# A short tile's residual by an accumulating transfer, and a later square for the thirteenth tile, in a gated encoder step

## Chip, cores and metric

The kernel runs on one core of a Trainium2 chip. The metric is the device time of one execution in microseconds (us); less is better. Five engines work side by side, each through its own queue of instructions in a fixed order: TensorE (PE, matrix products; PEld is its loading of weights), VectorE (DVE), ScalarE (ACT), GpSimd (POOL) and SyncE (SP, which here only issues transfers). GpSimd issues transfers too, among them those that add to what the destination holds ("accumulating transfers").

## The reference

One step of an encoder layer on 2048 rows of a new stream (the prompt) and 32 rows of a running one (the sample), of width D = 1024, in float32. The parts of `reference.py` that matter:

```python
def rmsnorm(x, g):
    x32 = x.astype(jnp.float32)
    y = x32 * lax.rsqrt(jnp.mean(x32 * x32, axis=-1, keepdims=True) + EPS)
    return (y * g.astype(jnp.float32)).astype(x.dtype)

def layer(h, p, conv_hist, pool_hist, pos, g_mix, w_in, conv_w, conv_b, pool_w, pool_scale,
          w_out, g_ple, w_ple_gate, w_ple):
    hn = rmsnorm(h, g_mix)
    proj = hn @ w_in
...
    h = h + jnp.concatenate([yA, yB], axis=-1) @ w_out
    gate = jax.nn.sigmoid(rmsnorm(h, g_ple) @ w_ple_gate)
    h = h + (p @ w_ple) * gate
    return h, new_conv, new_pool
...
    return rmsnorm(h, g_final), jnp.stack(convs, 0), jnp.stack(pools, 0)
```

Between `proj` and the output projection stand a short gated convolution (512 channels) and a pooling mixer (512 channels), whose last rows are returned as new states. The change concerns only the last two lines of the layer and the closing norm: `h + (p @ w_ple) * gate`, and `rmsnorm(h, g_final)`.

## The kernel before

**Tiles.** The rows are cut into sixteen tiles of 128 rows (0 to 15) and a short one of 32 rows, the sample (number 16, `NT - 1`). Each stage of the layer passes over all tiles and leaves its result in DRAM: `h_d` holds the rows after the output projection, `e_d` the product `p @ w_ple`. The change lies in the last stage, the gate stage, which runs from about 730 us to the end.

**Products.** A float32 product is made of three products of parts: `split` (lines 81 and 84) lets ScalarE cast a tile to its high part and VectorE subtract that from the tile, which leaves the low part, and `FINE` names the three pairs of parts that are multiplied. Two tiles of rows (a pair) go through `seven`, Strassen's scheme in Winograd's form: seven products of half tiles with half weights in place of eight, each of twelve matmuls of 128x128 by 128x512. In the first six of them stand the "steps" 1 to 6, at which other work is put into the program. The sums of rows that the scheme needs (S1 to S4) are made by `prep_g` for the next pair while this pair runs: VectorE transposes the two `hn` tiles (line 1560), then sums, then splits. Of each product, `carry` copies a first part out of PSUM (line 1573, ScalarE), and `out` adds the second (line 1581, VectorE), takes the sigmoid (line 1582, or 1579 where there is only one part), and multiplies `e` by it (line 1584, VectorE). Then comes `h`: line 1590 has GpSimd issue a transfer that adds the rows of `h_d` to `e` in place, so that `e` becomes the new `h`; where a tile's `h` has been loaded, VectorE adds `e` to it instead (line 1587).

**Closing norm.** `sumsq` (line 94, ScalarE) squares a finished tile and sums its rows, GpSimd turns the sum into the reciprocal root (lines 73 and 77), and `done_g` (line 1597, VectorE) scales the tile and sends it to the output (line 1600; GpSimd's queue, for tiles 12 to 15 SyncE's). `finishing` makes these four steps (square and scale of either tile) and the loop joins them to the steps 4, 5, 5 and 6 of the next pair.

**Order.** The loop takes the pairs 0, 2, ... 12 (named by their first tile); pair 14 is `last_pair`, in which the thirteenth tile (number 12) has its square at step 3 (`square0`) and its scale at step 4 (`scale0`); the last tiles are finished by hand in `end` (lines 1640 to 1667). After the pairs 0, 2 and 4 the short tile takes one step each: its load, its transposes and parts, its products (`plain`, without Strassen) with everything that follows them. A scheduler sorts the instructions of each engine; those that are marked `keep_in_program_order` (the squares and scales with `later=True`, the transposes, everything `fixed`) hold their order among themselves.

**Buffers.** Tiles come from rings, and an allocation waits for the last use of the tile that had the buffer. In the gate stage the ring `ya` has five buffers for the `e` of all pairs from 2 on and for the `e` of the short tile; the ring `xh` has six for the `hn` of the coming pairs (loaded by quarters, line 1512) and for an `h` that is loaded. Loads of `e` are line 396 on SyncE's queue. The names in the profile are those of the tiles; `x_g`, `y_g` and `z_g` are the PSUM banks of the seven products, `c_g` the copies, `x_gl` and `c_gl` those of the short tile.

Of the kernel before, what the change touches and what calls it, by code (L numbers as in the profile page):

```python
# [12 lines left out]
ALU = mybir.AluOpType  # L13
PSUM = bass.MemoryType.PSUM

P = 128
D = 1024
KC = D // P
SEQ = 2048
# [9 lines left out]
NT = SEQ // P + 1  # L29
# [7 lines left out]
def trunk(ctx, tc, x_p, x_s, c_conv, c_pool, p_p, p_s, g_mix, w_in, conv_w, conv_b, pool_w,  # L37
          pool_scale, w_out, g_ple, w_gate, w_ple, g_fin, y_p, y_s, sc_p, sp_p, sc_s, sp_s):
    nc = tc.nc
# [6 lines left out]
    h_d = tc.dram_tile([T, D], F32, name="h_d")  # L46
# [295 lines left out]
    def plain(name, A, W, n, carry, out):  # L342

        X, Y, Z = (bank(f"{c}_{name}") for c in "xyz")
        packed(X, A[0], W["11"], n, True)
        c2 = carry(X, (0, 1))
        packed(Z, A[0], W["T1"], n, True)
        packed(Z, A[1], W["22"], n, False)
        out(Z, c2, (0, 1))
        packed(X, A[1], W["21"], n, False)  # L350
        out(X, None, (0, 0))
# [41 lines left out]
    def load_rows(pool, name, i, pr, sa=None, queue=nc.sync):  # L393
        r, n = tiles[i]
        t = ring4(pool, f"{name}_{i}")
        queue.dma_start(t[:n], pr[r:r + n] if sa is None else rows_of(pr, sa, r, n))
        return t
# [906 lines left out]
    with ExitStack() as s2:  # L1304
# [263 lines left out]
        def gate_ops(h, e, n, name, i):  # L1568
            scale = lambda at: rs_h[:n, i + at[0]:i + at[0] + 1]

            def carry(ps, at):
                t = st.tile([P, NH], F32, tag="t", name=f"c_{name}_{at[0]}{at[1]}")
                carried.append(nc.scalar.copy(t[:n], ps[:n]))  # L1573
                return t

            def out(ps, c, at):
                if c is None:
                    c = st.tile([P, NH], F32, tag="t", name=f"g_{name}_{at[0]}{at[1]}")
                    nc.scalar.activation(c[:n], ps[:n], AF.Sigmoid, scale=scale(at))
                else:  # L1580
                    nc.vector.tensor_tensor(c[:n], ps[:n], c[:n], op=ALU.add)
                    nc.scalar.activation(c[:n], c[:n], AF.Sigmoid, scale=scale(at))
                ee = half_of(e, at, n)
                nc.vector.tensor_tensor(ee, ee, c[:n], op=ALU.mult)
                if h is not None and h[at[0]] is not None:
                    hh = half_of(h, at, n)
                    nc.vector.tensor_tensor(hh, hh, ee, op=ALU.add)
                elif at[0] + at[1] == 1:
                    r = tiles[i + at[0]][0]
                    nc.gpsimd.dma_start(e[at[0]], h_d[r:r + P], accum_op=ALU.add)  # L1590

            return carry, out
# [8 lines left out]

        def short_ops(h, e, n):

            carry1, out1 = gate_ops([h], [e], n, "gl", NT - 1)

            def carry(ps, at):
                t = carry1(ps, at)
                nc.vector.tensor_tensor(t[:n], ps[n:2 * n], t[:n], op=ALU.add)
                return t

            def out(ps, c, at):
                if c is None:
                    c = carry1(ps[n:2 * n], at)
                else:
                    nc.vector.tensor_tensor(c[:n], ps[n:2 * n], c[:n], op=ALU.add)
                out1(ps, c, at)

            return carry, out

        def last_pair(i, A, square0, scale0, square1, scale1):  # L1620
# [78 lines left out]
            def rest():  # L1699
                of_first(cols_of(0), nc.gpsimd)  # L1700
# [33 lines left out]
                weigh(1, cols_of(0))  # L1734
                normed(1, root(1))

            seven(f"g{i}", A, W, held, out, {1: lambda: (chunk(), square1()), 2: scale1, 3: square0, 4: lambda: (scale0(), rest()), 5: upper_half}, first_tile=True, end=end)

        def prep_g(i, ahead=False):

# [67 lines left out]
        def short_gate():  # L1808
            n = tiles[NT - 1][1]
            t = load_rows(ya, "hn", NT - 1, h_d)  # L1810
            yield
            A = short("gl", turned(NT - 1, t), n)
            h, e = (load_rows(*a) for a in ((xh, "h", NT - 1, h_d), (ya, "e", NT - 1, e_d)))
            yield
            plain("gl", A, W, n, *short_ops(h, e, n))
            done_g(NT - 1, h)
            yield

        def finishing(i, out):
            steps = []  # L1820
# [12 lines left out]
        def joined(a, b):  # L1833
            def both(p, q):
                def run():
                    p()
                    q()
                return run
            return {**a, **{st: both(a[st], f) if st in a else f for st, f in b.items()}}

        short_steps = short_gate()
        for i in range(0, NT - 3, 2):
            A = S.pop(i)
            following = prep_g(i + 2, not i)
            e = [load_rows(ya if i else xh, "e", i + b, e_d) for b in range(2)]
            h = [None, load_rows(xh, "h", i + 1, h_d)] if i == NT - 5 else None
            if i:
                for at, f in zip((4, 5, 5, 6), finish):
                    following = joined(following, {at: f})
            seven(f"g{i}", A, W, *gate_ops(h, e, P, f"g{i}", i), following)  # L1850
            finish = finishing(i, e if h is None else [e[0], h[1]])
            if i in (0, 2, 4):
                next(short_steps)
        last_pair(NT - 3, S[NT - 3], *finish)

# [27 lines left out]
```

## Time and profile before

| | |
|---|---|
| time, median of 3 runs | 907.2 us (907.12 to 908.23) |
| time of the profiled execution | 910.51 us |
| its span in the profile | 908.7 us, mean granted TensorE clock 0.996 |
| busy share of the span | PE 98%, PEld 79%, DVE 77%, ACT 50%, POOL 18% |
| moved by DMA | 198.51 MB, 218 GB/s over the span |
| gate stage | about 730 us to the end |
| TensorE's last product | ends at 901.4 us, 7.3 us ahead of the span's end |

The times of the runs are taken without the profiler; the profiled execution has a time of its own, and its span, from the first recorded instruction to the last, is what all positions below are counted in. A position such as 889.22 is in microseconds from the start of that span. A row of a timeline gives the start, the duration, the engine and line, the operation, the tiles written and read with their shapes, how many instructions were put together, and in brackets the idle time of the engine just before and what ended it. A row of the DMA view ends with the time from issue to landing. Matmuls overlap a little, so the durations of neighbouring rows add up to slightly more than the time between their starts.

### The profile page before, as it was taken

The page shows a single profiled execution, that of the slowest core. Times are in us where ns is not written, and L with a number is a line of the kernel's source. Part 1 is how long each engine was busy: PE and PEld are TensorE (multiplying, and loading weights), DVE is VectorE, ACT ScalarE, POOL GpSimd, SP SyncE. Part 2 cuts the span into 40 slices and gives each one's busy share as a digit, 9 for nine tenths or more (in the row PEclk, how much of TensorE's full clock was granted, in tenths as well). Part 3 has the DMA queues.
Part 4 walks back from the last instruction along what each step waited for, and adds up shares of the span by engine and source line. Part 5 has one row for each costly group of instructions (what it writes and reads, how often), then busy time and mean ns, then how long its engine had stood idle before and what let it go on. Part 6 is the DMA issues. An engine that isn't in the chain of part 4 may idle for free. (4 is left out here: it accounts for less than half of the span.)

```text
span 908.7 us, 12069 instructions
## 1 busy us (share of the span) xinstructions
PE 890.5 (98%) x4118; PEld 717.2 (79%) x4118; DVE 695.5 (77%) x1139; ACT 452.6 (50%) x820; POOL 166.5 (18%) x303
## 2 busy tenths in 40 slices
PE   8999999999999999999999999999999999999995
PEld 6788888888888888877788886888888788778884
DVE  6899799897993688846668579956466987688784
ACT  7744554554453354533444365544334865445453
POOL 2210122222121123100000020211111202214222
PEclk9999999999999999999999999999999999999998
DMA  8255286847699776667745496787677985698874
GB/s 273 57 188 173 83 259 204 248 157 225 178 339 427 174 225 196 215 222 235 255 137 172 164 343 192 251 256 259 204 261 271 306 264 116 155 216 228 219 212 176
DMA packets 116411, 198.51 MB, mean 218 GB/s; under 512 B 13510, under 2 KB 73982, under 8 KB 115453
## 3 DMA queue, kind: packets, MB, share of 16 engines
q1 hardware_dynamic: 92461, 117.91, 41.5%
q0 software_dynamic: 21440, 75.44, 26.6%
q10 hardware_dynamic: 2448, 4.39, 1.3%
q8 instruction: 32, 0.52, 0.2%
q14 instruction: 30, 0.25, 0.1%
HBM read 132.53 MB, written 65.15 MB: 218 GB/s over the span
## 5 line engine op out<-in xcount | busy, mean ns | idle before, releaser
L185 PE MATMUL z_g<-wg,g_S 128*128 128x512 f32 x192 | 48.1, 400 | 2.4 <-ACT c_g L1573 2.4
L185 PE MATMUL z_o<-wo,y_S 128*128 128x512 f32 x192 | 47.4, 389 | 0.0
L646 PE MATMUL x_zab<-B,w_zab_S 128*128 128x512 f32 x192 | 46.8, 391 | 0.2 <-DVE w_zab_S L84 0.2
L646 PE MATMUL z_zab<-B,w_zab_S 128*128 128x512 f32 x192 | 46.7, 391 | 0.0
L185 PE MATMUL x_o<-wo_T,y_S 128*128 128x512 f32 x192 | 46.5, 391 | 0.1
L185 PEld LDWEIGHTS z_g<-wg,g_S 128*128 128x128 f32 x192 | 36.4, 192 | 11.6 <-ACT c_g L1573 4.1
L185 PE MATMUL x_o<-wo,y 128*128 128x512 f32 x192 | 45.3, 390 | 0.1
L646 PEld LDWEIGHTS x_zab<-B,w_zab_S 128*128 128x128 f32 x192 | 35.8, 188 | 8.8 <-DVE w_zab_S L84 0.6
L185 PEld LDWEIGHTS x_o<-wo,y 128*128 128x128 f32 x192 | 36.0, 188 | 8.2 <-issue 0.5
L185 PEld LDWEIGHTS x_o<-wo_T,y_S 128*128 128x128 f32 x192 | 35.8, 188 | 8.3 <-DVE c_o L1319 0.9
L646 PEld LDWEIGHTS z_zab<-B,w_zab_S 128*128 128x128 f32 x192 | 35.8, 188 | 7.8 <-DVE w_zab_S L84 0.3
L185 PEld LDWEIGHTS z_o<-wo,y_S 128*128 128x128 f32 x192 | 36.0, 188 | 7.6 <-issue 0.2
L646 PE MATMUL x_ch<-B,w_ch_S 128*128 128x512 f32 x168 | 41.9, 392 | 0.0
L646 PE MATMUL x_zbv<-B,w_zbv_S 128*128 128x512 f32 x168 | 40.8, 392 | 0.0
L646 PE MATMUL z_zbv<-B,w_zbv_S 128*128 128x512 f32 x168 | 40.4, 390 | 0.0
L646 PE MATMUL z_ch<-B,w_ch_S 128*128 128x512 f32 x168 | 40.4, 389 | 0.0
L646 PEld LDWEIGHTS x_zbv<-B,w_zbv_S 128*128 128x128 f32 x168 | 31.3, 188 | 7.5 <-ACT V L986 0.4
L646 PEld LDWEIGHTS x_ch<-B,w_ch_S 128*128 128x128 f32 x168 | 31.3, 188 | 7.3 <-issue 0.4
L646 PEld LDWEIGHTS z_ch<-B,w_ch_S 128*128 128x128 f32 x168 | 31.5, 188 | 6.6
L646 PEld LDWEIGHTS z_zbv<-B,w_zbv_S 128*128 128x128 f32 x168 | 31.5, 188 | 6.5
L81 ACT CAST y_S<-y_fS 128x512 fp32r<-128x512 f32 x28 | 17.0, 619 | 26.3 <-PE x_o L185 12.2
L1373 POOL DMA_DIRECT2D gs<-in_w_ple_gate_dram x16 | 11.4, 716 | 87.9 <-DMA g_d<-gs 49.4
(559 smaller groups left out, 2271.5 us busy)
## 6 DMA issues: line engine op xcount, KB each, us to landing
wn<-in_w_in_dram SPq DMA_DIRECT2D x24, 512.0 KB, 5.0
y<-y_d SPq DMA_DIRECT2D x16, 512.0 KB, 7.0
hn<-h_d SPq DMA_DIRECT2D x61, 128.0 KB, 5.0
p_dT<-T POOLq DMA_DIRECT2D x15, 512.0 KB, 4.8
e<-e_d SPq DMA_DIRECT2D x15, 512.0 KB, 7.0
x<-in_x_prompt_dram SPq DMA_DIRECT2D x14, 512.0 KB, 5.3
e<-h_d POOLq DMA_DIRECT2D x13, 512.0 KB, 7.6
B<-p_d POOLq DMA_DIRECT2D x3, 2048.0 KB, 15.8
```

What stands on the lines that cost most here:

```text
L81: ins = nc.scalar.copy(hi, src)
L185: nc.tensor.matmul(ps[:n], lhs[:, k, a, :n], w[b][:, k], start=start and k + q == 0, stop=k == KH - 1 and q == 2, skip_group_check=True)
L646: nc.tensor.matmul(ps, lhs[:, k, x], b[:, k, y], start=start and k + q == 0, stop=stop and k == KH - 1 and q == 2, skip_group_check=True)
L1373: ins = nc.gpsimd.dma_start(t, rows[:, :, half * NH:half * NH + NH])
```

## The change

The short tile no longer loads its `h`. After its products an accumulating transfer adds the 32 rows of `h_d` to its `e`; its square goes into step 4 of pair 6, its scale and output into step 5 of that pair. The two additions of line 1587 with 32 rows are gone, and the `e` of the short tile is used a pair longer than before. In the last pair the square of tile 12 moves from step 3 to step 5, ahead of the gating of the last tile's upper half, and its scale from step 4 to step 6.

```diff
--- before.py
+++ after.py
@@ -1585,7 +1585,7 @@
                 if h is not None and h[at[0]] is not None:
                     hh = half_of(h, at, n)
                     nc.vector.tensor_tensor(hh, hh, ee, op=ALU.add)
-                elif at[0] + at[1] == 1:
+                elif n == P and at[0] + at[1] == 1:
                     r = tiles[i + at[0]][0]
                     nc.gpsimd.dma_start(e[at[0]], h_d[r:r + P], accum_op=ALU.add)
@@ -1601,7 +1601,7 @@
         def short_ops(h, e, n):
-            carry1, out1 = gate_ops([h], [e], n, "gl", NT - 1)
+            carry1, out1 = gate_ops(h, [e], n, "gl", NT - 1)
@@ -1734,7 +1734,7 @@
-            seven(f"g{i}", A, W, held, out, {1: lambda: (chunk(), square1()), 2: scale1, 3: square0, 4: lambda: (scale0(), rest()), 5: upper_half}, first_tile=True, end=end)
+            seven(f"g{i}", A, W, held, out, {1: lambda: (chunk(), square1()), 2: scale1, 4: rest, 5: lambda: (square0(), upper_half()), 6: scale0}, first_tile=True, end=end)
@@ -1810,11 +1810,11 @@
             A = short("gl", turned(NT - 1, t), n)
-            h, e = (load_rows(*a) for a in ((xh, "h", NT - 1, h_d), (ya, "e", NT - 1, e_d)))
-            yield
-            plain("gl", A, W, n, *short_ops(h, e, n))
-            done_g(NT - 1, h)
-            yield
+            e = load_rows(ya, "e", NT - 1, e_d)
+            yield
+            plain("gl", A, W, n, *short_ops(None, e, n))
+            nc.gpsimd.dma_start(e[:n], h_d[SEQ:], accum_op=ALU.add)
+            yield e
@@ -1847,10 +1847,14 @@
                 for at, f in zip((4, 5, 5, 6), finish):
                     following = joined(following, {at: f})
+            if i == 6:
+                rf, n = {}, tiles[NT - 1][1]
+                following = joined(following, {4: lambda: rf.update(r=sumsq(short_e, n, "fl", later=True)),
+                                               5: lambda: done_g(NT - 1, short_e, True, rf["r"])})
             seven(f"g{i}", A, W, *gate_ops(h, e, P, f"g{i}", i), following)
             finish = finishing(i, e if h is None else [e[0], h[1]])
             if i in (0, 2, 4):
-                next(short_steps)
+                short_e = next(short_steps)
```

Three places show how the order of the instructions changes. The first is SyncE's queue, where the loads for the pairs 6 to 12 are issued (`hn_8` is tile 8's `hn`, `e_8` its `e`; the last number of a name counts allocations; `x2` stands for so many quarters). Before:

```order
L1512 DMA hn_8_7132<-h_d_58 32x4x256 x2
L396 DMA e_6_7106<-e_d_59 128x1024
L1512 DMA hn_8_7132<-h_d_58 32x4x256 x2
L396 DMA e_7_7108<-e_d_59 128x1024
L1512 DMA hn_11_7295<-h_d_58 32x4x256
L396 DMA e_8_7274<-e_d_59 128x1024
L1512 DMA hn_11_7295<-h_d_58 32x4x256 x3
L1512 DMA hn_10_7300<-h_d_58 32x4x256 x4
L1512 DMA hn_13_7463<-h_d_58 32x4x256 x4
L396 DMA e_9_7276<-e_d_59 128x1024
L1512 DMA hn_12_7468<-h_d_58 32x4x256
```

And of the change:

```order
L1512 DMA hn_11_7292<-h_d_58 32x4x256 x2
L396 DMA e_6_7095<-e_d_59 128x1024
L1512 DMA hn_11_7292<-h_d_58 32x4x256
L396 DMA e_7_7097<-e_d_59 128x1024
L1512 DMA hn_11_7292<-h_d_58 32x4x256
L1512 DMA hn_10_7297<-h_d_58 32x4x256 x4
L1512 DMA hn_13_7460<-h_d_58 32x4x256 x4
L1512 DMA hn_12_7465<-h_d_58 32x4x256
L396 DMA e_8_7271<-e_d_59 128x1024
L1512 DMA hn_12_7465<-h_d_58 32x4x256 x2
L396 DMA e_9_7273<-e_d_59 128x1024
```

The loads of `e_6` and `e_7` now stand behind four more quarters of `hn`, and `e_8` comes behind all of `hn_10` and `hn_13` and the first quarter of `hn_12`. In the ring `ya`, `e_8` took the short tile's buffer before and `e_9` that of `e_4`; now `e_8` takes that of `e_4` and `e_9` the short tile's.

The second place is ScalarE's queue in the last pair (`c_g14` are the copies of pair 14, `e_12` is tile 12 with its gate and `h`, `h_14` the first tile of the last pair). Before:

```order
L1573 COPY c_g14_01_7852<-x_g14_7791 128x512
L94 ACTIVATE junk_90,ssq_f12_7854<-e_12_7610 128x1024
L1573 COPY c_g14_11_7872<-z_g14_7793 128x512
L1645 ACTIVATE junk_90,ssq_l0_0_7876<-h_14_7785 128x512
L1673 ACTIVATE c_g14_01_7852<-c_g14_01_7852,rs_h_88 128x512
L1673 ACTIVATE c_g14_11_7872<-c_g14_11_7872,rs_h_88 128x512
L1645 ACTIVATE junk_90,ssq_l0_512_7896<-h_14_7785 128x512
L1673 ACTIVATE g_l_7925<-x_g14_7791,rs_h_88 128x256
```

And of the change:

```order
L1573 COPY c_g14_01_7849<-x_g14_7788 128x512
L1573 COPY c_g14_11_7863<-z_g14_7790 128x512
L1645 ACTIVATE junk_90,ssq_l0_0_7865<-h_14_7782 128x512
L1673 ACTIVATE c_g14_01_7849<-c_g14_01_7849,rs_h_88 128x512
L1673 ACTIVATE c_g14_11_7863<-c_g14_11_7863,rs_h_88 128x512
L1645 ACTIVATE junk_90,ssq_l0_512_7885<-h_14_7782 128x512
L94 ACTIVATE junk_90,ssq_f12_7905<-e_12_7607 128x1024
L1673 ACTIVATE g_l_7922<-x_g14_7788,rs_h_88 128x256
```

The square of `e_12` went from ahead of the second copy to behind the second square of `h_14`, just ahead of the sigmoid of the last tile's lower half.

The third place is VectorE's queue at the end (`hg_0` is tile 14 on its way to the output, `h_15` the last tile). Before:

```order
L1597 SCALAR_TENSOR_TENSOR e_12_7610<-e_12_7610,rstd_f12_7858,g_bc_89 128x1024
L1677 TENSOR_TENSOR c_g14_01_7852<-z_g14_7793,c_g14_01_7852 128x512
L1640 TENSOR_TENSOR c_g14_01_7852<-e_14_7783,c_g14_01_7852 128x512
L1677 TENSOR_TENSOR c_g14_11_7872<-x_g14_7791,c_g14_11_7872 128x512
L1641 TENSOR_TENSOR h_14_7785<-h_14_7785,c_g14_01_7852 128x512
L1653 TENSOR_TENSOR hg_0_7789<-h_14_7785,g_bc_89 128x512
L1640 TENSOR_TENSOR c_g14_11_7872<-e_l512_7916,c_g14_11_7872 128x512
L1641 TENSOR_TENSOR h_15_7787<-h_15_7787,c_g14_11_7872 128x512
L1664 TENSOR_SCALAR hg_0_7789<-hg_0_7789,rstd_l0_7900 128x640
L1640 TENSOR_TENSOR g_l_7925<-e_l0_7939,g_l_7925 128x256
```

And of the change:

```order
L1677 TENSOR_TENSOR c_g14_01_7849<-z_g14_7790,c_g14_01_7849 128x512
L1640 TENSOR_TENSOR c_g14_01_7849<-e_14_7780,c_g14_01_7849 128x512
L1677 TENSOR_TENSOR c_g14_11_7863<-x_g14_7788,c_g14_11_7863 128x512
L1641 TENSOR_TENSOR h_14_7782<-h_14_7782,c_g14_01_7849 128x512
L1653 TENSOR_TENSOR hg_0_7786<-h_14_7782,g_bc_89 128x512
L1640 TENSOR_TENSOR c_g14_11_7863<-e_l512_7911,c_g14_11_7863 128x512
L1641 TENSOR_TENSOR h_15_7784<-h_15_7784,c_g14_11_7863 128x512
L1597 SCALAR_TENSOR_TENSOR e_12_7607<-e_12_7607,rstd_f12_7909,g_bc_89 128x1024
L1664 TENSOR_SCALAR hg_0_7786<-hg_0_7786,rstd_l0_7889 128x640
L1640 TENSOR_TENSOR g_l_7922<-e_l0_7936,g_l_7922 128x256
```

The scale of `e_12` stood ahead of all of this and now stands behind the first half of `h_15`, ahead of the scaling of `hg_0` and of the rest of the last tile.

## The prediction

> **What bounds the kernel now.** I read the page first, then the TensorE waits of the gate stage, then the two ends of each of them. The first view is the page's head.
>
> ```profile
> span 908.7 us, 12069 instructions
> ...
> PE 890.5 (98%) x4118; PEld 717.2 (79%) x4118; DVE 695.5 (77%) x1139; ACT 452.6 (50%) x820; POOL 166.5 (18%) x303
> ```
>
> TensorE is busy for 98% of the span, so time is lost or won only where it stands still, plus the tail behind its last product. The next view lists its waits from 700 us on, and the one after it is its timeline at the start of the last pair (tiles 14 and 15; columns: start, duration, engine and line, tiles, shapes, count, and in brackets the idle time ahead and who ended it).
>
> ```profile
> PE z_g L185 <- ACT c_g L1573: 2.4, 2, 2.2
> ...
> 885.93 1.07 PE L185 MATMUL x_g<-wg_T,g_S 128*128 128x512 f32 x4
> 889.22 4.29 PE L185 MATMUL z_g<-wg,g_S 128*128 128x512 f32 x12 [2.22 <-ACT c_g L1573]
> 893.31 2.34 PE L185 MATMUL x_g<-wg_T,g_S 128*128 128x512 f32 x8
> 895.48 1.52 PE L109 MATMUL e_l<-wl,pps_l 128*128 128x512 f32 x6
> ```
>
> The largest wait is one of 2.22 us ahead of the product of S4 and 22, ended by a copy of ScalarE on line 1573. ScalarE's own timeline says why that copy was late.
>
> ```profile
> 887.54 1.06 ACT L94 ACTIVATE junk<-e 128x1024 bf16<-128x1024 f32 x1 [3.55 <-DMA e<-h_d]
> ...
> 888.60 0.56 ACT L1573 COPY c_g<-z_g 128x512 f32<-128x512 f32 x1
> ```
>
> ScalarE stood for 3.55 us at the square of tile 12 (line 94), because the accumulating transfer into `e` had not landed; the copy is the next instruction in its queue. The square is what the second part of the change moves away. The wait costs more than its length: the twelve products behind it take from 889.22 to 893.31, 4.09 us, where twelve elsewhere take 2.72 us (834.16 to 836.88 in pair 8; a pair has seven such products). The last row below is that of the windows view for 891 to 893 us, where the granted clock is the number ahead of the last two.
>
> ```profile
> 819.60 2.88 PE L185 MATMUL y_g<-wg,g 128*128 128x512 f32 x12
> ...
> 834.16 2.88 PE L185 MATMUL x_g<-wq,g 128*128 128x512 f32 x12
> 836.88 2.43 PE L185 MATMUL x_g<-wg,g 128*128 128x512 f32 x10
> 839.14 2.88 PE L185 MATMUL y_g<-wg,g 128*128 128x512 f32 x12
> ...
> 891.00:893.00 2.00, 2.00 (x6) 1.54 (x6) 0.00 (x0) 0.00 (x0) 1.29 (x2) 0.50 0.98 401
> ```
>
> TensorE ran at half clock there, so the stall cost 2.22 + 1.37 = 3.6 us.
>
> **The change part by part.** Times below are put on the scale of this profile.
>
> *Pair 4 (tiles 4 and 5).* The short tile's `h` no longer takes a buffer of the ring that also holds the next pair's `hn`, so those loads start a slot earlier, and VectorE's wait for one goes.
>
> ```profile
> 783.95 1.25 DVE L1560 STREAM_TRANSPOSE hn<-hn 128x1024 f32<-128x1024 f32 x1 [4.83 <-DMA hn<-h_d]
> 785.12 0.65 DVE L1581 TENSOR_TENSOR c_g<-x_g,c_g 128x512 f32<-128x512 f32 x1
> ```
>
> VectorE's 4.83 us were idle time that TensorE did not feel: the product behind the sum at 785.12 started without a gap. In the new order that sum (L1581) stands behind four low-part subtractions (L84), which wait for as many casts on ScalarE, each like this one of pair 6:
>
> ```profile
> 815.78 0.62 ACT L81 CAST g<-hn 128x512 fp32r<-128x512 f32 x1
> ```
>
> I get the sum some 0.8 us later, and a wait of 0.8 us on TensorE. Against it the wait of 0.6 us at the short tile's second product goes, since VectorE has caught up. Bounds -0.6 and +0.9 us; I take 0.
>
> *Pair 6.* Three things that stood ahead of its work leave VectorE: two additions of 32x512 ahead of the row below, and the scale of the short tile, which waited for GpSimd.
>
> ```profile
> 805.31 1.27 DVE L1597 SCALAR_TENSOR_TENSOR h<-h,rstd_f,g_bc 32x1024 f32<-32x1024 f32 x1 [1.59 <-POOL rstd_f L77]
> ...
> 807.11 1.23 DVE L1560 STREAM_TRANSPOSE hn<-hn 128x1024 f32<-128x1024 f32 x1
> ...
> 799.61 2.91 PE L185 MATMUL y_g<-wg,g 128*128 128x512 f32 x12
> ...
> 815.82 3.04 PE L185 MATMUL x_g<-wq,g 128*128 128x512 f32 x12 [0.60 <-DVE c_g L1581]
> ```
>
> The transpose at 807.11 came 4.6 us behind the end of the y product (802.5); in pair 8 it comes 2.4 us behind (824.91, in a row below, against 822.5). So the chain moves about 2.4 us ahead and the wait of 0.60 us at 815.82 goes: with the restart 0.7 us, and pair 8's y product starts at 818.9 in place of 819.60. That pair takes 839.14 - 819.60 = 19.54 us for 7 x 2.72 = 19.04 us of products; the 0.5 us go too if its order holds. Gain 1.2 us. The bound on the other side is none: tile 6's `e` is loaded about a microsecond ahead of its use now.
>
> *The price: the load of tile 8's `e`.* The short tile's `e` lives a pair longer, and the five buffers of that ring are handed on by the last use. Before, tile 8's `e` took the buffer that the short tile had left in pair 4. Now it takes tile 4's, and its load must wait until tile 4's output has left. These are the `e` loads on SyncE's queue before, then GpSimd's queue, then the time from issue to landing of the transfers at 820.95, 824.05, 829.42 (tile 10's load) and 806.65.
>
> ```profile
> 807.57 0.38 SPq L396 DMA_DIRECT2D e<-e_d  x1
> ...
> 824.05 0.34 SPq L396 DMA_DIRECT2D e<-e_d  x1
> ...
> 820.95 0.63 POOL L1600 DMA_DIRECT2D out_dram<-e  x1
> 821.57 0.92 POOL L1590 DMA_DIRECT2D e<-h_d  x1
> ...
> 823.21 0.86 POOL L1590 DMA_DIRECT2D e<-h_d  x1
> ...
> out_dram<-e POOLq DMA_DIRECT2D x1, 512.0 KB, 3.1
> ...
> e<-e_d SPq DMA_DIRECT2D x1, 512.0 KB, 9.7
> ...
> e<-e_d SPq DMA_DIRECT2D x1, 512.0 KB, 6.4
> ...
> e<-e_d SPq DMA_DIRECT2D x1, 512.0 KB, 4.9
> ```
>
> Tile 8's load was issued at 807.57, 17 us ahead of its use. The load at 824.05 is tile 9's, the one that already waited for tile 4's output (820.95 + 3.1 = 824.05): it landed 9.7 us later, beside two accumulating transfers. Now tile 8 is in that place, and tile 8 is needed a whole half pair sooner than tile 9. When is tile 4's output issued? Tile 4's scale stood on VectorE at 818.70, and its output on GpSimd behind the next tile's root (820.11 to 820.95):
>
> ```profile
> 818.70 1.28 DVE L1597 SCALAR_TENSOR_TENSOR e<-e,rstd_f,g_bc 128x1024 f32<-128x1024 f32 x1
> ...
> 820.11 0.88 POOL L77 TENSOR_TENSOR rstd_f<-ms_f,nhalf 128x1 f32<-128x1 f32 x1
> ```
>
> The scale moves 1.7 to 2.4 us ahead with pair 6's chain, and the output no longer waits for that root. That gives 817.6 to 818.6; I take 818.1, landing at 821.2, and with it the issue of tile 8's load. Landing 4.9 to 9.7 us later gives 826.1 to 830.9. Two accumulating transfers run then as well, so I take 8.1, the mean of this load and the next one (6.4): 829.3.
>
> Who stands behind it? VectorE's queue is strict, and the product that needs tile 8's `e` is ahead of both transposes of the next pair.
>
> ```profile
> 824.91 1.24 DVE L1560 STREAM_TRANSPOSE hn<-hn 128x1024 f32<-128x1024 f32 x1
> ...
> 832.89 0.68 DVE L1581 TENSOR_TENSOR c_g<-x_g,c_g 128x512 f32<-128x512 f32 x1
> ```
>
> From the first transpose (824.91) to the end of the sum (832.89 + 0.68) VectorE is packed for 8.66 us; behind a load at 829.3 and the product (0.6) the sum ends at 838.6. TensorE needs that sum for the product that stood at 834.16: from 818.9, four products (10.9) bring it to 829.8, S4 x 22 to 832.5, and the six products of the next pair now put ahead of it to 833.9. It waits 838.7 - 833.9 = **4.8 us**; bounds 1.6 and 6.4 us.
>
> A stop of that length, cut only by six products, is longer than the 2.22 us behind which the clock was halved, so I add that row's **1.4 us**; its lower bound is 0. The Trainium skill ("TensorE: Matmul & The Clock Gate", section "Why this matters for your kernels") advises against TensorE gaps above about 3 us; by that alone a gap cut into pieces under 3 us would keep the clock, and the sum would be 1.4 us less. This trace differs: its gap was 2.22 us and the clock fell to 0.50, and the row decides.
>
> *Last pair.* Without the square the copy can run when its product ends (886.1), so S4 x 22 starts at 887.0 in place of 889.22 and at full clock: `e_l` starts 12 + 8 products of 0.227 later, at 891.5 in place of 895.48. Not all of these 3.9 us reach the end. The square, its root on GpSimd and tile 12's scale on VectorE now stand in the tail, ahead of the first tile's scaling and of the last tile's `h`.
>
> ```profile
> 893.55 0.69 DVE L1677 TENSOR_TENSOR c_g<-z_g,c_g 128x512 f32<-128x512 f32 x1 [2.63 <-PE z_g L185]
> ...
> 898.34 0.69 DVE L1641 TENSOR_TENSOR h<-h,c_g 128x512 f32<-128x512 f32 x1
> 898.94 0.55 DVE L1664 TENSOR_SCALAR hg<-hg,rstd_l 128x640 f32<-128x640 f32 x1
> 899.41 0.42 DVE L1640 TENSOR_TENSOR g_l<-e_l,g_l 128x256 f32<-128x256 f32 x1
> ...
> 901.99 0.43 DVE L1641 TENSOR_TENSOR h<-h,g_l 128x256 f32<-128x256 f32 x1
> ```
>
> With the sum of 893.55 at 890.0, ScalarE reaches the square at 894.2 (two sigmoids, one half square), ends it at 895.3, and GpSimd has the root at 896.3 (1.0 us later, from the 0.88 of the row at 820.11). VectorE, which has been idle since the `h` of 898.34 (now 894.7 to 895.4), then scales tile 12 for 1.28 us (the row at 818.70), scales the first tile (0.55), and reaches the work of 899.41 at 898.0. The five steps to the last `h` take 1.85 us, so the row of 901.99 starts at 899.9. Gain **2.1 us**, 1.8 of the 3.9 being given back. Behind it nothing changes. Bounds 0 (tile 12's scale late by as much again) and 3.9.
>
> The sum: 0 - 1.2 + 4.8 + 1.4 - 2.1 = **+2.9 us**. The profiled execution, 910.51 us for a span of 908.7, would become 913.4 and its span 911.6. It is 3.3 us above the median of the runs shown (907.2), and I carry the difference over: 907.2 + 2.9 = **910.1 us**.
>
> **The rivals.** *The load slips in between (faster).* One mechanism decides: how soon tile 8's `e` lands. At 4.9 us (826.1) TensorE waits only 1.6 us, the clock holds, and the sum is -1.2 + 1.6 - 2.1 = -1.7 us, 905.5; with no wait at all it is -3.3, 903.9. For it speaks the row of 4.9 us; against it, that this load had no accumulating transfer in progress beside it. The Trainium skill ("DMA: Bandwidth & Descriptors", section "Queues, rings and completion order") says that each DMA engine takes turns between rings by packet, by which the load would start beside the first accumulation and land early; the 9.7 us of the row at 824.05 show a longer wait than that. It becomes faster than I can tell only for landings before about 826.
>
> *A middling landing (no change).* At 6.4 us, as the load after it took, it lands at 827.6: wait 3.1 us, no halved clock for certain, sum -0.2 to +1.2, 907.0 to 908.4.
>
> *Everything goes ahead of it.* If both accumulations and tile 5's output pass first, it lands after 831.5: wait 7 us, clock halved, sum +5.2, 912.4. Four `hn` quarters of pair 4, issued from 773.64 on, speak for a wait this long: they took 8.7 us.
>
> ```profile
> hn<-h_d SPq DMA_DIRECT2D x4, 128.0 KB, 8.7
> ```
>
> *The change does not do what it says.* If the sum of tile 12's square is late in its new place too, the 2.1 us are 0 and my forecast is 912.2.
>
> **How the numbers follow.** Chances: forecast 0.46, no change 0.26, faster 0.15, the later landing or the lost tail 0.13. About 0.2% (1.8 us) is what a measurement of this kernel tells from no change: slower (above 909.0) gets 0.59, within 0.26, faster (below 905.4) 0.15. The range for 8 in 10 runs from 905.4 (the early landing's edge) to 912.6 (the late one); the forecast's own is 908.8 to 911.6, from landings between 828 and 830.9.
>
> **What would show it.** Tile 8's load of `e` issued near 821 and landing near 829; VectorE idle ahead of the product on line 1584 in pair 8, ended by that transfer; TensorE waiting for the sum of line 1581 near 834 for 3 us or more in all, with a window at clock 0.5 behind it; no wait ahead of S4 x 22 in the last pair; VectorE idle about 1 us in the tail ahead of tile 12's scale. A load that lands before 826 makes the forecast wrong in sign, and a wait of TensorE in pair 4 or 6 above 1 us makes the first terms wrong.

## The result, and the profile after

The changed kernel took 911.58 us (median of 4 runs, 910.6 to 912.72) beside 907.48 us for the kernel before (4 runs): a ratio of 1.0042, with a 95% interval of 1.0026 to 1.0058, or 2.4 to 5.3 us more. Measured again beside 23 runs of before, it stood at 912.56 against 909.58 us, a ratio of 1.0027 (1.0011 to 1.0043). It is slower, as forecast.

The head of the page of the changed kernel alone would not tell so: its span is only 0.1 us longer than that of before (908.7).

```profile
span 908.8 us, 12064 instructions
...
PE 890.0 (98%) x4118; PEld 717.5 (79%) x4118; DVE 694.2 (76%) x1137; ACT 452.8 (50%) x820; POOL 169.7 (19%) x304
```

That is chance ahead of the stage in question. The instructions of both kernels come in the same order up to the gate stage, and yet its first y product starts at 733.15 us in the profile of before and at 731.20 in this one. So the profiles are compared from there on. The table gives the time from a pair's y product to that of the next pair, for the last pair to the end of the span, and for the whole gate stage from the first y product to the end; each is a difference of two starts in the timeline of TensorE (us).

| profile | pair 4 | pair 6 | pair 8 | last pair | gate stage |
|---|---|---|---|---|---|
| before | 27.53 | 19.99 | 19.54 | 30.97 | 175.59 |
| the change | 27.71 | 19.37 | 24.35 | 28.62 | 177.61 |
| difference | +0.18 | -0.62 | +4.81 | -2.35 | +2.02 |

The pairs 0, 2, 10 and 12 take the same in both to 0.01 us. TensorE's waits of the changed kernel from 700 us on show where pair 8 lost its time (total, times, longest), and the timeline shows the place.

```profile
PE x_g L185 <- DVE c_g L1581: 2.8, 2, 2.4
PE x_g L185 <- DVE g L84: 0.5, 1, 0.5
```

```profile
832.12 1.20 PE L185 MATMUL x_g<-wg,g 128*128 128x512 f32 x4 [0.55 <-DVE g L84]
835.73 4.60 PE L185 MATMUL x_g<-wq,g 128*128 128x512 f32 x12 [2.41 <-DVE c_g L1581]
840.17 1.55 PE L185 MATMUL x_g<-wg,g 128*128 128x512 f32 x6
```

The copy of ScalarE that headed the list before is gone from it. In its place stands VectorE's sum (line 1581), 2.41 us at one place in pair 8, with 0.55 us just ahead of it for a low part (line 84). The twelve products behind it run from 835.73 to 840.17, 4.44 us where 2.72 are normal; the window of 837 to 839 us has the clock at one half (the number ahead of the last two).

```profile
837.00:839.00 2.00, 2.00 (x6) 1.59 (x5) 2.00 (x3) 1.58 (x3) 0.95 (x1) 0.50 0.47 177
```

VectorE was late because of the load of tile 8's `e`. First VectorE, then the queues of SyncE and GpSimd, then the times from issue to landing of the output at 816.53 and the accumulating transfer at 817.53:

```profile
826.40 0.69 DVE L1584 TENSOR_TENSOR e<-e,c_g 128x512 f32<-128x512 f32 x1 [3.13 <-DMA e<-e_d]
827.01 1.24 DVE L1560 STREAM_TRANSPOSE hn<-hn 128x1024 f32<-128x1024 f32 x1
...
834.99 0.68 DVE L1581 TENSOR_TENSOR c_g<-x_g,c_g 128x512 f32<-128x512 f32 x1
```

```profile
819.62 0.34 SPq L396 DMA_DIRECT2D e<-e_d  x1
```

```profile
816.53 0.64 POOL L1600 DMA_DIRECT2D out_dram<-e  x1 [1.62 <-DVE e L1597]
...
817.53 0.91 POOL L1590 DMA_DIRECT2D e<-h_d  x1
...
820.47 0.90 POOL L1590 DMA_DIRECT2D e<-h_d  x1
```

```profile
out_dram<-e POOLq DMA_DIRECT2D x1, 512.0 KB, 3.0
```

```profile
e<-h_d POOLq DMA_DIRECT2D x1, 512.0 KB, 5.8
```

Tile 4's output went at 816.53 and landed 3.0 us later; at 819.62 SyncE issued the load that waited for it, behind one accumulating transfer and ahead of another; at 826.40, 6.8 us later, VectorE could multiply. The transposes follow at once, and the sum that TensorE needs starts 8.6 us after the product. The whole chain stands 9.2 us behind pair 8's y product (817.21); before, that product started at 824.30, 4.7 us behind it.

In the last pair the products of S4 and 22 start without a wait and run at full clock, and the scale of tile 12 is in the tail, where VectorE waits 0.94 us for its root:

```profile
889.25 3.02 PE L185 MATMUL z_g<-wg,g_S 128*128 128x512 f32 x12
```

```profile
897.11 0.69 DVE L1641 TENSOR_TENSOR h<-h,c_g 128x512 f32<-128x512 f32 x1
898.75 1.29 DVE L1597 SCALAR_TENSOR_TENSOR e<-e,rstd_f,g_bc 128x1024 f32<-128x1024 f32 x1 [0.94 <-POOL rstd_f L77]
899.95 0.55 DVE L1664 TENSOR_SCALAR hg<-hg,rstd_l 128x640 f32<-128x640 f32 x1
```

### The profile page after: what moved, and what is told of

Its sections match the earlier page's. It is cut to its first block, busy times and chain, and to the rows that moved or that the text cites. A ratio compares the mean times of both kernels' runs of the same rounds, so it can differ in the third digit from the quotient of the medians.

```text
span 908.8 us, 12064 instructions
## 1 busy us (share of the span) xinstructions
PE 890.0 (98%) x4118; PEld 717.5 (79%) x4118; DVE 694.2 (76%) x1137; ACT 452.8 (50%) x820; POOL 169.7 (19%) x304
```

## The experiments

All were run beside the kernel before on the same chip. The times of one kernel scatter by 2 to 9 us in these sets. In the profiles the start of the gate stage differs by up to 5.9 us (731.0 to 736.9) between kernels that are alike up to there, while the segments of one kernel agree far better, so both are given. In the table the ratio is that to before, with its interval; two kernels were run only once, so their single times stand there. The last three lines are versions whose times lie below those of both kernels.

| kernel | pair 4 | pair 6 | pair 8 | last pair | gate stage | ratio of times |
|---|---|---|---|---|---|---|
| before, again | 27.10 | 19.97 | 19.57 | 30.71 | 174.91 | 0.9998 (0.9978 to 1.0018) |
| change, again | 27.27 | 19.37 | 24.41 | 28.62 | 177.24 | 1.0027 (1.0011 to 1.0043) |
| short tile alone | 27.25 | 19.39 | 24.65 | 29.33 | 178.20 | 1.0073 (1.0061 to 1.0085) |
| short tile alone, again | 27.37 | 19.41 | 23.81 | 28.96 | 177.12 | 1.0058 (1.0037 to 1.0079) |
| last pair alone | 27.02 | 19.97 | 19.57 | 28.81 | 172.94 | 0.9995 (0.9981 to 1.0010) |
| buffer apart | 27.62 | 19.30 | 20.45 | 28.62 | 173.55 | 0.9991 (0.9977 to 1.0004) |
| held early (run once) | 27.96 | 19.97 | 19.85 | 30.30 | 175.63 | 912.34 us |
| held late (run once) | 26.96 | 19.97 | 22.63 | 30.60 | 178.33 | 914.18 us |
| square between | 27.09 | 19.97 | 19.55 | 28.08 | 172.25 | 0.9976 (0.9962 to 0.9990) |
| norm moved, h kept | 27.10 | 19.12 | 19.31 | 27.17 | 170.27 | 0.9953 (0.9935 to 0.9971) |
| norm moved, square between | 27.68 | 19.11 | 19.31 | 28.08 | 171.73 | 0.9960 (0.9947 to 0.9973) |

### Before, once more

No edit.

> The kernel before, unchanged, profiled anew. Its profiled execution took 910.51 us, 3.0 us above the median of its runs, and holds the stall of 2.22 + 1.37 us in the last pair. Theory A (the stall is in every execution): the wait ahead of S4 x 22 in the last pair is 2 us or more again, with a window at half clock, and the time of this profiled execution is whatever the rest of the program makes it. Rival B (the stall belongs to that one execution, and the timed ones run without it): the profiled execution takes about 907.5 us and shows a wait under 1 us there; then the second part of the change had nothing to win in the timed runs.

Neither came out as a whole. The wait is there again, 1.94 us with half clock behind it:

```profile
886.38 4.61 PE L185 MATMUL z_g<-wg,g_S 128*128 128x512 f32 x12 [1.94 <-ACT c_g L1573]
```

But this profiled execution took 907.74 us, no more than the timed ones. So theory A holds for the stall (all six profiles with tile 12's square in its old place have a wait of 1.8 to 2.4 us there, four of them with half clock behind it), and the 3 us by which the first profiled execution lay above its median do not come from there: 2.1 us of them lie ahead of the gate stage (its first y product at 733.15, here at 731.02).

### The short tile alone

The change, with the last pair as before:

```diff
-            seven(f"g{i}", A, W, held, out, {1: lambda: (chunk(), square1()), 2: scale1, 4: rest, 5: lambda: (square0(), upper_half()), 6: scale0}, first_tile=True, end=end)
+            seven(f"g{i}", A, W, held, out, {1: lambda: (chunk(), square1()), 2: scale1, 3: square0, 4: lambda: (scale0(), rest()), 5: upper_half}, first_tile=True, end=end)
```

> Only the first part: the short tile's accumulating transfer and its square and scale in pair 6; tile 12 as before. My theory: the load of tile 8's e lands late and TensorE stands in pair 8 for 3.0 us and runs at half clock for 1.7 us behind it, pair 4 +0.2, pair 6 -0.6, so +4.4 us against before, 911.9 us. Rival (most of the loss comes from the last pair's new order, the tail): about +2, 909.5 us or less. The profile should show tile 8's load issued behind the output of tile 4 and VectorE idle for some 3 us ahead of line 1584 in pair 8.

Pair 8 lost what was expected, 24.65 us, from the same waits of 0.54 and 2.42 us, and VectorE stood 3.43 us for the transfer ahead of line 1584. The rival falls with that: the loss is there with the last pair as in before. The gate stage grew by 3.0 us over the mean of the two profiles of before (175.25), and not by the 4.4 I expected, since in its last pair a wait of 2.36 us was not followed by half clock. The time grew by more, 6.1 us (915.54 against 909.39). The rest is ahead of the gate stage, in the output projection:

```profile
664.38 4.57 PE L185 MATMUL z_o<-wo,y_S 128*128 128x512 f32 x12 [2.73 <-DVE c_o L1319]
```

```profile
656.37 0.72 ACT L1379 ACTIVATE gs<-gs,vec 128x512 f32<-128x512 f32 x1 [4.50 <-DVE c_o L1319]
...
660.90 0.72 ACT L1379 ACTIVATE gs<-gs,vec 128x512 f32<-128x512 f32 x1 [3.80 <-DMA gs<-in_w_ple_gate_dram]
```

ScalarE waited for a load of the gate weight (line 1379) until 660.90, where before had it at 656.38; TensorE then stood 2.73 us and ran at half clock. The order of instructions there is the same as in before. A second measurement was to tell whether that belongs to this program.

> The first part alone, once more. All its runs took 914.9 to 916.9 us, and 4.4 us of the profiled one were lost near 662 us, ahead of the gate stage, where a load of a weight (line 1379) was 4 us later than elsewhere. Theory (that was chance): 910 to 912 us this time, no such wait, gate stage 178.2 us. Rival (it belongs to that program, whatever its gate stage does): 915 us again with the wait at the same place.

Its profile has no such wait and a gate stage of 177.1 us, so the stall near 662 us is not in every execution. But its ten runs spread from 908.99 to 917.80 us with a median of 915.13. Whether the long ones meet that stall was not profiled, and why this program takes longer than its gate stage explains stays open. The gate stage is the sounder measure of this part: +1.9 and +3.0 us.

### The last pair alone

The kernel before with the other half of the diff (the first line above in place of the second).

> Only the second part: tile 12's square at step 5 and its scale at step 6; the short tile as before. Theory A (the stall of the last pair is in every execution of before): -2.3 us, 905.2 us. Rival B (it is in few of them): the removed wait brings nothing, and tile 12's scale, which now stands ahead of the last tile's h in the tail, costs 0 to 1.4 us: 907.5 to 908.9 us.

The gate stage took 172.94 us, 2.3 us less than before, and the last pair 28.81, as in the change; TensorE's waits have no entry of the copy above 0.2 us:

```profile
PE x_g L185 <- DVE c_g L1581: 0.6, 1, 0.6
...
PE z_g L185 <- ACT c_g L1573: 0.2, 1, 0.2
```

The times do not confirm the size: 0.9995 (0.9981 to 1.0010) is anything from 1.7 us less to 0.9 us more. Theory A's 2.3 us (a ratio of 0.9975) lie just outside that, rival B's lower end inside. So the gain of the stage is shown, and its worth in time is not.

### The short tile's buffer apart

```diff
-            e = load_rows(ya, "e", NT - 1, e_d)
+            e = load_rows(xh, "e", NT - 1, e_d)
```

> The changed kernel, but the short tile's e takes a buffer of the ring xh (where its h was before) and not of ya, so that tile 8's e does not wait for tile 4's output. My theory (the lost time is that load): the 4.7 us of pair 8 go, 911.6 - 4.7 = 906.9 us, with tile 8's load issued before 812 and no wait above 0.6 us in pair 8. Rival 1 (the accumulating transfer itself, or the short tile's norm in pair 6, holds TensorE up): no gain, 911 us or more. Rival 2 (the wait moves to tile 9's load, or to hn loads that lack the buffer): a wait of 1 to 3 us in pair 6 or 8 stays, 908 to 910 us.

This is the change in all but the ring of one tile. Tile 8's load goes at 805.92, and of the 4.8 us that pair 8 lost 0.9 are left. These are SyncE's row, TensorE's and VectorE's:

```profile
805.92 0.34 SPq L396 DMA_DIRECT2D e<-e_d  x1
```

```profile
834.15 3.01 PE L185 MATMUL x_g<-wq,g 128*128 128x512 f32 x12 [1.11 <-DVE c_g L1581]
```

```profile
820.70 1.27 DVE L1597 SCALAR_TENSOR_TENSOR e<-e,rstd_fl,g_bc 32x1024 f32<-32x1024 f32 x1 [1.65 <-POOL rstd_fl L77]
...
823.63 1.28 DVE L1597 SCALAR_TENSOR_TENSOR e<-e,rstd_f,g_bc 128x1024 f32<-128x1024 f32 x1 [1.06 <-POOL rstd_f L77]
...
825.43 1.24 DVE L1560 STREAM_TRANSPOSE hn<-hn 128x1024 f32<-128x1024 f32 x1
```

The accumulating transfer, the moved square and the moved scale are all still there, so rival 1 falls. What is left is a smaller effect: VectorE waits 1.65 us for the short tile's root and 1.06 us for tile 5's, and the transposes come 6.6 us behind the y product (818.82), where before has 5.3. TensorE waits 1.11 us for the sum. The ratio is 0.9991 (0.9977 to 1.0004): against the 1.0027 of the change in the next set, the loss is gone. The gate stage says 173.55, 3.9 us less than the change. Rival 2 is right in its size, a wait of 1.11 us left in pair 8 and 908.38 us, but not in its cause: VectorE waits for no load there, only for roots. Part of that lateness is in the change too (waits of 1.65 and 1.04 us for the same two roots), hidden there behind the later load. My 906.9 us was missed, with before at 909.39 in this set.

### The buffer held, and nothing else

Two kernels leave the short tile as in before and keep its `e` in use, early or late in pair 6, by one instruction on it that the result does not need (the square of the early one brings its small root on GpSimd with it).

```diff
             done_g(NT - 1, h)
-            yield
+            yield e
...
+            if i == 6:
+                following = joined(following, {5: lambda: sumsq(short_e, DEC, "fl", later=True)})
...
-                next(short_steps)
+                short_e = next(short_steps)
```

In the late one the added line is

```diff
+                following = joined(following, {6: lambda: tc.keep_in_program_order(nc.vector.tensor_scalar(short_e[:DEC], short_e[:DEC], scalar1=1.0, scalar2=None, op0=ALU.mult))})
```

> The kernel before with one thing more: a square of the short tile's e (32 rows, its sum is not used) in step 5 of pair 6, so that its buffer in the ring ya comes free only there; no accumulating transfer, nothing moved. Tile 8's e waits for it. My theory: what counts is when the load lands. Released about 817 to 819, ahead of the accumulating transfers of that pair (821.6 in before), it lands some 5 us later, before 825, and pair 8 stays at 19.5 to 20.5 us. Rival (any load issued this late is caught behind the accumulating transfers): it lands after 828, and pair 8 takes 22 us or more.

> As the run with the early hold, but the short tile's e is held by a multiplication by 1 on VectorE in step 6 of pair 6, about 821 to 823 us, by when tile 4's output and the accumulating transfer of tile 6 have been issued. My theory: tile 8's load then lands 8 to 10 us later, 830 to 833 us, and pair 8 takes 19.3 + (2 to 6) + 1.7 us, 23 to 27 us, without any other part of the change. Rival (the loss of the change needs its accumulating transfer of 32 rows or the moved norm): pair 8 below 20.5 us.

Early: the load went at 822.99, 1.2 us behind pair 8's y product and ahead of both accumulating transfers of that time; VectorE multiplied at 827.42, 4.4 us later, and pair 8 took 19.85 us, as my theory has it (the 0.3 us more is a wait of 0.51 us for the sum). Counted from pair 8's y product the load went 2 to 4 us later than I had expected: 1.2 us behind it, where 817 to 819 in before is 0.6 to 2.6 us ahead of it.

```profile
822.99 0.34 SPq L396 DMA_DIRECT2D e<-e_d  x1
```

```profile
836.75 3.02 PE L185 MATMUL x_g<-wq,g 128*128 128x512 f32 x12 [0.51 <-DVE c_g L1581]
```

Late: the load went at 823.28 (the first of the two in its row), behind one accumulating transfer (821.93), and VectorE stood 5.70 us, until 830.16, 6.9 us later and 10.2 us behind the y product.

```profile
823.28 1.41 SPq L396 DMA_DIRECT2D e<-e_d  x2
```

```profile
830.16 0.69 DVE L1584 TENSOR_TENSOR e<-e,c_g 128x512 f32<-128x512 f32 x1 [5.70 <-DMA e<-e_d]
```

Pair 8 took 22.63 us, with 0.63 us more in pair 10. No other part of the change is in this kernel, so a buffer handed on late is enough to cost pair 8 some 3 us; the rival falls. My range of 23 to 27 us was missed by a little, for a reason that TensorE's rows show:

```profile
834.60 0.73 PE L185 MATMUL x_g<-wg,g 128*128 128x512 f32 x2 [0.89 <-ACT g L81]
835.88 2.33 PE L185 MATMUL x_g<-wg,g 128*128 128x512 f32 x9 [0.55 <-DVE g L84]
839.49 3.02 PE L185 MATMUL x_g<-wq,g 128*128 128x512 f32 x12 [1.28 <-DVE c_g L1581]
```

The stop came in three waits of 0.89, 0.55 and 1.28 us, with eleven products of the next pair put between them, and the clock held: the product behind the last one takes its 3.02 us.

### The change, once more

No edit.

> The changed kernel again, beside the same runs of before as the others. In the two profiles of before the gate stage (from the first y product of pair 0 to the end) takes 175.6 and 174.9 us, in that of the change 177.6. My theory: the same again, 177.6 +- 0.5 us, with pair 8 at 24.3 and the last pair at 28.6 us, and the timed runs 2.4 us above before. Rival (something ahead of the gate stage is slower in the changed kernel too): a first y product later than 733.5 us, and 4 us or more.

177.24, 24.41 and 28.62 us: these two segments and pair 6 come back to 0.1 us, pair 4 and the gate stage only to 0.4. The first y product stands at 732.22, so nothing ahead of the stage is slower, and the time is 2.5 us above before (1.0 to 3.9). Pair 8 has the same two waits, 0.54 and 2.42 us.

### Tile 12's square between the two places

```diff
-            seven(f"g{i}", A, W, held, out, {1: lambda: (chunk(), square1()), 2: scale1, 3: square0, 4: lambda: (scale0(), rest()), 5: upper_half}, first_tile=True, end=end)
+            seven(f"g{i}", A, W, held, out, {1: lambda: (chunk(), square1()), 2: scale1, 4: lambda: (rest(), square0(), scale0()), 5: upper_half}, first_tile=True, end=end)
```

> The kernel before with tile 12's square moved by one step only, to step 4 behind the first half square of tile 14, and its scale behind it in the same step, so that it stands behind the copy on line 1573 but not in the tail. My theory: the last pair takes 30.8 us in before and 28.6 to 28.8 with the change, of which 0.9 us of VectorE's wait for tile 12's root plus part of the 1.28 us of its scale lie in the tail; here they go, and the last pair takes 27.4 to 27.9 us, the timed runs 2 to 3 us less than before. Rival (the accumulating transfer lands so late that the scale holds up the sums behind it): 28.5 us or more.

It is faster than before (0.9976, 0.9962 to 0.9990), and the last pair is 0.5 to 0.7 us shorter than with the change, but not by as much as I expected: 28.08 us. The scale stands where VectorE had nothing to do, and still ends too late:

```profile
893.33 1.29 DVE L1597 SCALAR_TENSOR_TENSOR e<-e,rstd_f,g_bc 128x1024 f32<-128x1024 f32 x1 [5.21 <-POOL rstd_f L77]
894.53 0.68 DVE L1677 TENSOR_TENSOR c_g<-z_g,c_g 128x512 f32<-128x512 f32 x1
...
896.62 0.68 DVE L1677 TENSOR_TENSOR c_g<-x_g,c_g 128x512 f32<-128x512 f32 x1
```

```profile
897.35 1.70 PE L1722 MATMUL x_g<-wq,g 128*128 128x256 f32 x12 [1.06 <-DVE c_g L1677]
```

Two sums on line 1677 stand behind it in VectorE's queue, and the second frees the bank that the half products of the last tile need; TensorE stands 1.06 us. So the scale does hold up the sums, as the rival has it, though at less than its price. That the transfer is the reason is not shown: the square waited 0.52 us for it here, and in the last kernel below, where it waits only 0.18 us, the last pair takes the same 28.08 us.

### Norm moved, h kept

The short tile as before (its `h` loaded, its two additions) but its norm later, and the last pair with the scale a step behind the square:

```diff
             plain("gl", A, W, n, *short_ops(h, e, n))
-            done_g(NT - 1, h)
-            yield
+            yield h
...
+            if i == 6:
+                rf, n = {}, tiles[NT - 1][1]
+                following = joined({2: lambda: rf.update(r=sumsq(short_h, n, "fl", later=True))}, following)
+                following = joined(following, {5: lambda: done_g(NT - 1, short_h, True, rf["r"])})
...
-                next(short_steps)
+                short_h = next(short_steps)
...
-            seven(f"g{i}", A, W, held, out, {1: lambda: (chunk(), square1()), 2: scale1, 3: square0, 4: lambda: (scale0(), rest()), 5: upper_half}, first_tile=True, end=end)
+            seven(f"g{i}", A, W, held, out, {1: lambda: (chunk(), square1()), 2: scale1, 4: lambda: (rest(), square0()), 5: lambda: (scale0(), upper_half())}, first_tile=True, end=end)
```

> The short tile keeps its loaded h and the two additions, so that its e is free as early as before; its square goes into step 2 and its scale into step 5 of pair 6. In the last pair tile 12's square stands in step 4 behind the first half square of tile 14, its scale in step 5. My theory: tile 8's load is issued early again; pair 6 takes 19.4 us (it lost 0.6 us to the short tile's scale), pair 8 19.5 us, the last pair 27.2 to 28.0 us against 30.8; gate stage 171.5 to 172.2 us. Rival 1 (the short tile's scale on VectorE in pair 6 delays pair 8's transposes, as where its buffer was apart): pair 8 20.3 us or more. Rival 2 (the moved norm is what cost the change its time): pair 8 22 us or more.

904.90 us against 909.04 for before: 0.9953 (0.9935 to 0.9971), the fastest of all. Every segment is at or below the lower bound I gave (pair 6 at 19.12, pair 8 at 19.31, the last pair at 27.17), the gate stage 5.0 us below that of before. TensorE has a single wait left in it (the first row); VectorE scales the short tile and then tile 5 without a wait, since the short square was done long before; and in the last pair tile 12's scale finds its root ready:

```profile
PE x_gl L337 <- DVE c_gl L1608: 0.5, 1, 0.5
```

```profile
818.30 1.27 DVE L1597 SCALAR_TENSOR_TENSOR h<-h,rstd_fl,g_bc 32x1024 f32<-32x1024 f32 x1
...
820.10 1.27 DVE L1597 SCALAR_TENSOR_TENSOR e<-e,rstd_f,g_bc 128x1024 f32<-128x1024 f32 x1
```

```profile
891.94 0.68 DVE L1641 TENSOR_TENSOR h<-h,c_g 128x512 f32<-128x512 f32 x1
892.54 1.28 DVE L1597 SCALAR_TENSOR_TENSOR e<-e,rstd_f,g_bc 128x1024 f32<-128x1024 f32 x1
```

Rival 2, the moved norm as the cause, falls here as it did where the buffer stood apart: this kernel moves the norm too and loses nothing. Rival 1 falls as well; what cost 1.1 us there was a square too late for its scale, not the scale, which takes its 1.27 us on VectorE here as well.

> As the run before it in the short tile; in the last pair tile 12's square and scale both in step 4, as in the run with the square between. In that run the scale waited for the transfer and held the sum behind it, and TensorE stood 1.06 us for it. My theory: the last pair takes 28.0 us again, 0.3 to 0.8 us more than with the scale in step 5. Rival (a scale in the tail costs as much as one that holds the sum): no difference above 0.2 us.

Its only difference is the step of `scale0` (4 in place of 5). The last pair takes 28.08 us, 0.91 more, a little over my range, with a wait of 1.08 us for the sum as in the run before; the times (0.9960 against 0.9953) cannot tell the two apart.

## Why the prediction was right, point by point

The sign, the place and the mechanism were right; of the terms, those for pair 6 and for the load were mis-sized, and that their errors partly cancel is luck. The measured values are means of the two profiles of each kernel.

- **Pair 4: taken as 0.** Measured +0.2 us (27.49 against 27.32), less than the two profiles of before differ from each other (0.43). The wait for the sum that I named (0.8 us) is in one profile of the change with 0.42 us and not in the other; the wait at the short tile's second product did not go, but fell from 0.62 and 0.47 us to 0.32 in both.
- **Pair 6: taken as -1.2, measured -0.6.** The wait of 0.60 us went, as said. The other half I took from pair 8's 19.54 us, on the condition that its order holds; it does not, since that pair now waits. Where nothing waits, pair 6 takes 19.12 and pair 8 19.31 us (norm moved, h kept), so about 1.1 of the 1.2 us were there to be had.
- **The load of tile 8's `e`: taken as +4.8 and +1.4, measured +4.8 in all.** The issue was predicted 2.3 us behind pair 8's y product (821.2 against 818.9); it came 2.4 behind (819.62 against 817.21). The landing was mis-sized: I took 8.1 us from issue; by the end of VectorE's wait it took 6.8, close to the 6.4 of my rival with the middling landing. (826.40 is not the early landing that would have made the sign wrong: it stands 9.2 us behind the y product, which on the forecast's scale, with that product at 818.9, is 828.1.) The path behind it was right: VectorE is packed for 8.66 us from the first transpose to the end of the sum, as in before. TensorE waited 2.96 us, not 4.8. The clock was taken at 1.4 us and cost 1.7 (12 products in 4.44 us). The six products that I let run ahead of the waiting one did not all fill the time: four of them waited for the same late chain (0.55 us, part of the 2.96).
- **The last pair: taken as -2.1, measured -2.2** (28.62 against 30.84). This was not luck: behind the pair's y product the square of tile 12 starts 16.5 us (896.65), where I had 16.4, and the last `h` of line 1641 stands 22.1 us (902.26), as I had it. The 0.94 us that VectorE waits for tile 12's root in the tail is part of what I gave back.
- **The sum:** predicted +2.9 us, measured +2.2 in the gate stage (177.43 against 175.25), +3.8 and +2.5 by the ratios of the times, whose intervals overlap from 2.4 to 3.9. What made the first of these larger than the stage explains was not found. I carried the difference onto the median of the runs shown; 2.1 us of the 3 us that the profiled execution took more lay ahead of the stage, and so did not belong to the change.

Of the rivals, the middling landing was nearest in its condition: 3.1 us of waiting against 2.96. It had the clock as not certain to drop and the gain of pair 6 whole, and so came to no change at 907.0 to 908.4. The clock did drop, in all four profiles with the short tile's part and the late load, and that and the half gain of pair 6 decided the sign. The lost tail did not come. The rule of the Trainium skill on gaps ("TensorE: Matmul & The Clock Gate", "Why this matters for your kernels") would have kept the clock at these 0.55 and 2.41 us; the windows show 0.50, so the row was the better guide. The rule of the Trainium skill on turns between the queues ("DMA: Bandwidth & Descriptors", "Queues, rings and completion order") would have had the load land early, beside the transfer in progress; it took 6.8 us behind one, against 4.4 us where it was issued ahead of them, so some waiting is shown, less than I took.

One statement on the kernel has to be put right: the ring `xh` has four buffers (line 1306), not six. No term hangs on it.

## What to carry to other kernels

When a tile of a ring lives longer, look which later tile inherits its buffer, and count that tile's load from the moment of release: here a gain of some 2.8 us at two places was outweighed by one load that had been issued 17 us ahead of its use and now came 14 us later against the pair that needs it. Before moving a finishing step to hide it, move its parts separately: the reduction as early as its input allows, the scaling into a gap of the engine that does it, and neither in front of a copy that releases the bound engine. Where single executions scatter by several us ahead of the stage that was changed, compare that stage between two landmarks of the profile; here the segments of one kernel came back to 0.1 to 0.4 us, and to 0.8 us at worst (pair 8 of the short tile alone), while the times of most kernels spread over 3 us and more.

## What had not been expected

**The clock.** From 640 us on in these profiles, every single wait of TensorE up to 1.69 us left the clock at full speed, and ten of twelve between 1.81 and 2.73 us were followed by half clock, the next twelve products taking 4.1 to 4.5 us. The two exceptions are in the last pair of the short tile's part alone, where waits of 2.36 and 1.95 us left it at full:

```profile
897.34 3.02 PE L185 MATMUL z_g<-wg,g_S 128*128 128x512 f32 x12 [2.36 <-ACT c_g L1573]
```

```profile
892.98 3.06 PE L185 MATMUL z_g<-wg,g_S 128*128 128x512 f32 x12 [1.95 <-ACT c_g L1573]
```

Both lie some 56 us behind an earlier half-clock stretch (pair 8's), which no other wait of the list does; whether that is the reason was not tried. It is also why the last pair of that kernel took 29.0 to 29.3 us and not 30.8.

**A stall by chance far ahead.** The part of the gate weight that ScalarE scales on line 1379 near 655 us is there for it between 654.4 and 660.9 us in these profiles, with the same instructions ahead of it, and TensorE stands for 0 to 2.73 us behind it. The kernel with the square between has such a wait at another place as well (2.13 us at 692.23, followed by half clock). Runs of the kernel before lie between 906.0 and 916.2 us in these sets; how much of that spread comes from these places was not measured.
